# The first weight unit of a two-layer decoder by pairs of feature tiles, and the norm's weights on ScalarE's queue

## The chip, the cores and the metric

The kernel runs as one program on 1 core of one Trainium2 chip. The metric is device time in microseconds (us) of one execution; the kernel before was run three times and its median is used. Times inside an execution are counted from the start of the profiled span. PE is TensorE, ACT ScalarE, DVE VectorE, POOL GpSimd, SP SyncE; SP's queue issues nearly all transfers.

## What is computed

Two layers of a hybrid decoder over 256 tokens of 1024 features, in float32. Each layer is a half SwiGLU block, a token mixer (windowed attention beside a gated recurrence in layer 0, a chunked delta rule in layer 1), cross-attention into 256 memory tokens, and another half SwiGLU block, each behind an RMSNorm. The part that the change touches is the very first block:

```python
def rmsnorm(x, g):
    y = x * rsqrt(mean(x * x, axis=-1, keepdims=True) + 1e-6)
    return y * g

def swiglu(h, w_in, w_out):              # w_in: 1024 x 5632, w_out: 2816 x 1024
    gate, up = split(h @ w_in, 2, axis=-1)
    return (silu(gate) * up) @ w_out

x = x + 0.5 * swiglu(rmsnorm(x, ffn1_norm[0]), ffn1_w_in[0], ffn1_w_out[0])
```

## The kernel before

Every weight matrix is cut into units of 256 columns by up to 1024 rows (eight feature tiles k of 128). A unit is loaded in two halves of four tiles, 512 KB each, into a ring of `RAW` = 5 raw buffers (`load_to`), and each half is split (`split_half`, lines 158 and 159): ACT copies the weights rounded into `wt[..., 0, :]`, the high part, and DVE subtracts that from the raw weights to get the low part `wt[..., 1, :]`. Activations are kept transposed, features on partitions, and split in the same way: `x2[:, k, 0]` high and `x2[:, k, 1]` low.

`mm3` makes one product of a unit's column half j (128 columns) over some tiles k. For each k it issues two matmuls: `high` (line 200), the weights' high part against both parts of the activations side by side, 512 columns wide, and `low` (line 204), the weights' low part against the activations' high part, 256 columns wide. For the last k the low comes first. A pair in the texts below is one high with its low; a unit has 16 of them. Eight tiles accumulate in one PSUM bank per j. Outside the start, `tick` splits the next half while a unit's products run, and a list `plan` with its `queue` of halves sets the order of the weights. Line 271 (`add`) and line 270 then fold a finished bank's two halves together in SBUF.

The start is in `setup`, inside `tc.manual_schedule()`: there each engine issues its instructions in the order written. Outside that region the scheduler orders them, by its own estimate of what is ready when.

- The gains of the first norm are read as rows into `dcw` (128 rows of 512 B, line 467, on SP's queue), transposed on PE (line 483) and copied to `gains` (line 484).
- x comes in four pieces of 256 features, 256 KB each, into `xs` (lines 473 and 477). For each piece c, `transposed` (line 429) makes four transposes on PE, and `take` (lines 503 and 506) multiplies by the gains and splits: ACT makes the high part of both feature tiles, DVE the low part. The mean of squares is not needed for this: its reciprocal root is applied after the products.
- `idle(n)` (line 491) issues n matmuls of a matrix of ones that nobody reads.
- The loads stand in this order on SP's queue: dcw, x's pieces 0 and 1, unit 0's first half (in two transfers), unit 1's first half, x's pieces 2 and 3, then the second halves of units 0 and 1, then unit 2's first half. The queue of halves is swapped for this (line 75).
- PE's order: `idle(7)`, the gains, piece 0's transposes, `idle(3)`, piece 1's transposes, `idle(6)`, unit 0's products over tiles 0 to 3, the transposes of pieces 2 and 3, unit 1's over 0 to 3, then the second halves of both units.
- Behind the products ACT squares x with a running sum (line 535), DVE copies the transposed x from PSUM to `xT` (line 537) and scales the sums to `ms` (line 366), POOL takes the power -1/2 into `rcol` (line 341), and PE transposes that to a row (`stats_rows`, line 374). These transposes stand on PE behind the products of units 0 and 1 and ahead of unit 2.

Of the kernel before, what the change touches and what calls it, by code (L numbers as in the profile page):

```python
# [9 lines left out]
F32 = mybir.dt.float32  # L10
# [3 lines left out]
AF = mybir.ActivationFunctionType  # L14
# [4 lines left out]
P = 128  # L19
S = 256  # L20
D = 1024
KD = 8
# [45 lines left out]
class Net:  # L68
    def __init__(self, tc, t):
        self.tc, self.nc, self.t = tc, tc.nc, t  # L70
        self.raws, self.halves = {}, {}
        self.plan = list(self.make_plan())
        self.queue = [(i, k) for i, u in enumerate(self.plan) for k in range(0, u[4], 4)]

        self.queue[1], self.queue[2] = self.queue[2], self.queue[1]
        self.n_load = self.n_half = self.n_take = 0
        self.later = deque()
        self.banks, self.n_bank = "w", 0
        self.now, self.due = 0, []
# [46 lines left out]
            yield from four("xa_wo", l)  # L126
            yield from ffn(2, l)

    def load_to(self, n, step=4):

        nc = self.nc
        while self.n_load < min(n, len(self.queue)):
            i, k = self.queue[self.n_load]
            name, l, c0, k0, nk, cols = self.plan[i]
            m = min(4, nk - k)
            raw = self.p_raw.tile([P, 4, 256], F32, name="raw")
            src = self.t[name][l, (k0 + k) * P:(k0 + k + m) * P, c0:c0 + cols]
            src = src.rearrange("(k p) c -> p k c", p=P)
            for u in range(0, m, step):
                us = slice(u, min(m, u + step))  # L140
                nc.sync.dma_start(raw[:, us, :cols], src[:, us])
            self.raws[self.n_load] = raw
            self.n_load += 1

    def split_half(self, step=4):

        nc = self.nc
        i, k = self.queue[self.n_half]
        name, l, _, _, nk, cols = self.plan[i]
        self.load_to(self.n_half + 1)  # L150
        n = min(4, nk - k)
        wt = self.p_wt.tile([P, 4, 2, 256], F32R, name="wt")
        raw = self.raws.pop(self.n_half)
        self.n_half += 1
        for u in range(0, n, step):
            us = slice(u, min(n, u + step))
            a, b, r = wt[:, us, 0, :cols], wt[:, us, 1, :cols], raw[:, us, :cols]
            nc.scalar.activation(a, r, AF.Copy)  # L158
            nc.vector.tensor_sub(b, r, a.bitcast(F32))  # L159
        self.halves.setdefault(i, []).append(wt)  # L160

    def w(self, name, c0):

# [23 lines left out]

    def mm3(self, out, wts, cols, mov, ks, k0=0, start=0, stop=KD):  # L190

        nc = self.nc
        for k in ks:
            i = k - k0
            w = wts[i // 4][:, i % 4]

            def high():
                nc.tensor.matmul(out.rearrange("p a s -> p (a s)"), w[:, 0, cols], mov[:, k].rearrange("p a s -> p (a s)"),  # L200
                                 start=k == start, stop=k == stop - 1)

            def low():
                nc.tensor.matmul(out[:, 0], w[:, 1, cols], mov[:, k, 0], start=False, stop=False)  # L204

            for part in (low, high) if k == stop - 1 else (high, low):
                part()

# [223 lines left out]
    def setup(self, ctx):  # L432
        nc, tc, t = self.nc, self.tc, self.t
# [8 lines left out]
        c = self.p_c  # L442
# [11 lines left out]
        self.dcw = c.tile([P, P], F32, name="dcw")  # L454

        warm = c.tile([P, 1], F32, name="warm")
        nc.scalar.activation(warm, self.ones[:, :1], AF.Silu)
        x_pool = tc.tile_pool(name="xs", bufs=1, reuse_waits="tile")
        xs = x_pool.__enter__().tile([P, 2, D], F32, name="xs")
        x = t["x"][0].rearrange("(t p) d -> p t d", p=P)  # L460
        spare = self.p_sm.tile([P, S], F32, name="acc", bufs=2)
        rows0, rows, rows2 = self.dcw, spare[:, :P], spare[:, P:]

        def put(dst, r0, name, eng, n=None, times=1):
            ap = t[name]
            n = n or math.prod(ap.shape) // P
            eng.dma_start(dst[r0:r0 + n * times],
                          bass.AP(tensor=ap.tensor, offset=ap.offset, ap=[[0, times], [P, n], [1, P]]))

        put(rows0, 0, "ffn1_norm", nc.sync, times=8)  # L470

        for a, b in ((0, 256), (256, 512)):
            nc.sync.dma_start(xs[:, :, a:b], x[:, :, a:b])
        self.load_to(1, 2)
        self.load_to(2)
        for a, b in ((512, 768), (768, 1024)):
            nc.sync.dma_start(xs[:, :, a:b], x[:, :, a:b])
        self.load_to(RAW)
        xs = [xs[:, j] for j in range(2)]

        def columns(dst, src, which="s"):
            ps = self.bank(which)
            nc.tensor.transpose(ps[:, 0, :P], src, self.ident)
            nc.vector.tensor_copy(dst, ps[:, 0, :P])

        with tc.manual_schedule():

            def idle(n):
                ps = self.bank("w").rearrange("p a s -> p (a s)")
                for _ in range(n):  # L490
                    nc.tensor.matmul(ps[:, :P], self.ones, self.ones, start=True, stop=True)

            idle(7)
            gains = self.p_sm.tile([P, 1, S], F32, name="bc", bufs=2)[:, 0, :P]
            columns(gains, rows0, "w")
            banks = []

            def take(ks, ps):
                banks.append((ks, ps))
                g = lambda k: gains[:, C_FFN1 + k:C_FFN1 + k + 1]  # L500
                for j in range(2):
                    k = ks.start + j
                    nc.scalar.activation(self.x2[:, k, 0], ps[:, j], AF.Copy, scale=g(k))
                for j in range(2):
                    k = ks.start + j
                    nc.vector.scalar_tensor_tensor(self.x2[:, k, 1], ps[:, j], g(k), self.x2[:, k, 0].bitcast(F32),
                                                   op0=OP.mult, op1=OP.subtract)


            self.first = [[self.bank(w) for w in u] for u in ("ww", "ws")]  # L510

            def products(u, half, j):
                self.mm3(self.first[u][j], self.halves[u], slice(j * P, j * P + P), self.x2,
                         range(4 * half, 4 * half + 4))

            self.transposed(xs, take, (0,))
            idle(3)
            self.transposed(xs, take, (1,))
            idle(6)
            self.split_half(2)  # L520
            products(0, 0, 0)
            self.split_half()
            products(0, 0, 1)
            self.transposed(xs, take, (2, 3))
            products(1, 0, 0)
            products(1, 0, 1)
            for u in range(2):
                self.split_half(2)
                for j in range(2):
                    products(u, 1, j)  # L530
            self.load_to(4 + RAW)
            ms = self.p_sm.tile([P, 2], F32, name="ms", bufs=2)
            for j in range(2):
                junk = self.m2[:, 2 * j:2 * j + 2].rearrange("p k a s -> p (k a s)")
                nc.scalar.activation(junk, xs[j], AF.Square, accum_out=ms[:, j:j + 1])
            for ks, ps in banks:
                nc.vector.tensor_copy(self.xT[:, ks], ps)
# [939 lines left out]
```

## Time and profile before

| | |
|---|---|
| three runs | 1252.36, 1251.72 and 1255.6 us, median 1252.36 |
| profiled execution | 1251.99 us, its span 1250.2 us |
| PE busy | 1236.0 us, 99% of the span |
| DVE, ACT, POOL busy | 929.0, 752.0 and 80.5 us |
| moved by DMA | 222.92 MB, mean 178 GB/s |
| mean granted TensorE clock | 0.998 |

A row of a timeline has the start in us, the duration in us, the engine, the line of the kernel, the operation, output and input, and how many like instructions are merged in the row; in brackets stand the idle time of the engine ahead of it and what ended that. Matmuls overlap, so a row's duration is longer than its distance to the next. A row of a waits view has who waited for whom, the total in us, the number of times and the longest. A row of the DMA issues has the count, the size of one and, where the trace has it, the median time in us from issue to landing.

### The profile page before, as it was taken

The numbers are of one execution on the slowest core, as the hardware profiler recorded it, in microseconds if no ns is written. First come the engines' busy times: TensorE is split into PE (matmuls) and PEld (weight loads), VectorE is DVE, ScalarE is ACT, GpSimd is POOL, SyncE is SP. The second block draws the span as 40 slices with busy tenths as digits, with TensorE's granted clock in tenths as the row PEclk, the third lists the DMA queues.
The fourth block names the chain that finished last, engine by engine and source line by source line (L and its number), as shares of the span: only waits on it lengthen the run. The fifth ranks groups of instructions, "written<-read, shape, count | busy, mean of one in ns | idle before, by whom it ended". The sixth has DMA issues, their size and how long they took to land.

```text
span 1250.2 us, 20300 instructions
## 1 busy us (share of the span) xinstructions
PE 1236.0 (99%) x7702; PEld 1104.9 (88%) x7702; DVE 929.0 (74%) x1590; ACT 752.0 (60%) x1281; POOL 80.5 (6%) x96
## 2 busy tenths in 40 slices
PE   9999999999999999999999999999999999999997
PEld 8888889888998888888888888888898998888887
DVE  6987957788668778766877756989757668777753
ACT  7766545886555665545656544776757465666543
POOL 1000020000101000011000001020001101000000
PEclk9999999999999999999999999999999999999999
DMA  8766676544544566557666566667534535666561
GB/s 272 215 206 197 185 255 185 178 125 152 185 135 154 185 198 184 183 185 231 187 187 195 181 192 204 183 153 193 142 99 135 181 124 169 185 186 194 177 194 60
DMA packets 231019, 222.92 MB, mean 178 GB/s; under 512 B 14969, under 2 KB 228617, under 8 KB 230793
## 3 DMA queue, kind: packets, MB, share of 16 engines
q1 hardware_dynamic: 229448, 217.94, 56.9%
q0 software_dynamic: 1152, 3.15, 1.0%
q8 instruction: 60, 0.98, 0.3%
q10 hardware_dynamic: 320, 0.53, 0.1%
q14 instruction: 39, 0.31, 0.1%
HBM read 215.03 MB, written 5.51 MB: 176 GB/s over the span
## 4 chain that ended last, share of the span: by engine, by line
PE 90%; DVE 5%; ACT 2%; DMA 1%; issue 1%; POOL 1%; ACTq 0%; DVEq 0%; POOLq 0%
PE psw L200 21%; PE pss L200 16%; PE psw L204 11%; PE psf L200 11%; PE pss L204 8%; PE psf L204 5%; PE psw L242 5%; PE psf L242 4%; PE pss L242 3%; PE psw L216 2%; DVE wt L159 1%; PE psw L220 1%; ACT wt L158 1%; PE pss L1268 1%; PE psf L1274 1%
## 5 line engine op out<-in xcount | busy, mean ns | idle before, releaser
L159 DVE TENSOR_TENSOR wt<-raw,wt 128x1024 fp32r<-128x1024 f32 (+1 forms) x409 | 484.9, 1191 | 202.8 <-ACT wt L158 199.6
L158 ACT ACTIVATE wt<-raw 128x1024 fp32r<-128x1024 f32 (+1 forms) x409 | 418.6, 1031 | 172.1 <-PE psw L204 59.4
L200 PE MATMUL psw<-x,wt 128*128 128x512 f32 x864 | 310.6, 396 | 2.1 <-DVE xn L271 1.8
L204 PE MATMUL psw<-x,wt 128*128 128x256 f32 x864 | 224.9, 281 | 0.5 <-DVE wt L159 0.5
L200 PE MATMUL pss<-x,wt 128*128 128x512 f32 x520 | 187.4, 393 | 0.0
L200 PEld LDWEIGHTS psw<-x,wt 128*128 128x128 f32 x864 | 160.6, 188 | 30.1 <-issue 2.1
L204 PEld LDWEIGHTS psw<-x,wt 128*128 128x128 f32 x864 | 162.4, 188 | 9.4 <-DVE wt L159 1.0
L204 PE MATMUL pss<-x,wt 128*128 128x256 f32 x520 | 134.9, 280 | 0.0
L200 PE MATMUL psf<-x,wt 128*128 128x512 f32 x352 | 127.2, 394 | 0.0
L200 PEld LDWEIGHTS pss<-x,wt 128*128 128x128 f32 x520 | 97.7, 188 | 16.9 <-ACT bc L377 0.4
L204 PEld LDWEIGHTS pss<-x,wt 128*128 128x128 f32 x520 | 97.7, 188 | 5.4
L200 PE MATMUL psw<-h,wt 128*128 128x512 f32 x264 | 94.9, 396 | 0.0
L204 PE MATMUL psf<-x,wt 128*128 128x256 f32 x352 | 91.3, 280 | 0.0
L200 PE MATMUL pss<-h,wt 128*128 128x512 f32 x242 | 87.0, 396 | 0.0
L336 POOL TENSOR_TENSOR acc<-acc,sq 128x256 f32<-128x256 f32 x49 | 43.7, 891 | 658.3 <-ACT sq L334 557.3
L200 PEld LDWEIGHTS psf<-x,wt 128*128 128x128 f32 x352 | 66.1, 188 | 11.2
L204 PE MATMUL psw<-h,wt 128*128 128x256 f32 x264 | 72.0, 280 | 0.0
L204 PEld LDWEIGHTS psf<-x,wt 128*128 128x128 f32 x352 | 66.2, 188 | 3.5
L204 PE MATMUL pss<-h,wt 128*128 128x256 f32 x242 | 66.0, 280 | 0.0
L200 PEld LDWEIGHTS psw<-h,wt 128*128 128x128 f32 x264 | 49.6, 188 | 10.8
L200 PE MATMUL psf<-h,wt 128*128 128x512 f32 x154 | 55.4, 397 | 0.0
L200 PEld LDWEIGHTS pss<-h,wt 128*128 128x128 f32 x242 | 45.5, 188 | 9.8
(377 smaller groups left out, 2109.2 us busy)
## 6 DMA issues: line engine op xcount, KB each, us to landing
raw<-in_ffn_w_in_dram SPq DMA_DIRECT2D x175, 512.0 KB, 3.6
raw<-in_ffn_w_out_dram SPq DMA_DIRECT2D x80, 512.0 KB, 3.6
raw<-in_xa_wkv_dram SPq DMA_DIRECT2D x32, 512.0 KB, 3.5
raw<-in_dn_w_in_dram SPq DMA_DIRECT2D x32, 512.0 KB, 4.6
raw<-in_ab_w_in_dram SPq DMA_DIRECT2D x20, 512.0 KB, 3.6
raw<-in_xa_wq_dram SPq DMA_DIRECT2D x16, 512.0 KB, 3.5
raw<-in_xa_wo_dram SPq DMA_DIRECT2D x16, 512.0 KB, 3.4
raw<-in_ffn_w_out_dram SPq DMA_DIRECT2D x16, 256.0 KB, 2.9
```

What stands on the lines that cost most here:

```text
L158: nc.scalar.activation(a, r, AF.Copy)
L159: nc.vector.tensor_sub(b, r, a.bitcast(F32))
L200: nc.tensor.matmul(out.rearrange("p a s -> p (a s)"), w[:, 0, cols], mov[:, k].rearrange("p a s -> p (a s)"), start=k == start, stop=k == ...
L204: nc.tensor.matmul(out[:, 0], w[:, 1, cols], mov[:, k, 0], start=False, stop=False)
L216: nc.tensor.matmul(out.rearrange("p a s -> p (a s)"), mov[:, k, 0, tok], w.rearrange("p a s -> p (a s)"), start=k == 0, stop=k == KD - 1)
L220: nc.tensor.matmul(out[:, 0], mov[:, k, 1, tok], w[:, 0], start=False, stop=False)
L242: self.nc.tensor.matmul(out, a[u], b[w], start=first and i == 0, stop=last and i == 2)
L336: (eng or nc.gpsimd).tensor_add(self.acc, self.acc, sq)
L1268: nc.tensor.matmul(py[:, i], na[:, i], tu[:, 0, i], start=True, stop=True)
L1274: nc.tensor.matmul(pp[:, i], yy[:, i], tu[:, 1, i], start=True, stop=True)
```

## The change

`load_pair(n)` loads two feature tiles (256 KB) of unit 0, and `setup` now alternates: x's piece n, then the weights' tiles 2n and 2n + 1, for n from 0 to 3. Unit 1's halves and unit 2's first half follow; the swap of the queue is gone, so a unit's halves are neighbours. The splits become a generator, `split_steps`, which gives control back after each piece of two tiles. PE's order becomes: `idle(5)`, the gains, piece 0's transposes, `idle(3)`, and then three times the transposes of the next piece and the products of the pair of tiles before it over both j, and behind them the last pair; with `late=True` the four highs of a pair stand before its four lows. Unit 1 follows as two whole halves, each split in one piece. `idle(6)` is gone. The load of `dcw` moves from SP's queue to ACT's, ahead of the activation that warms up ACT's table.

```diff
--- before.py
+++ after.py
@@ -71,8 +71,6 @@
         self.raws, self.halves = {}, {}
         self.plan = list(self.make_plan())
         self.queue = [(i, k) for i, u in enumerate(self.plan) for k in range(0, u[4], 4)]
-
-        self.queue[1], self.queue[2] = self.queue[2], self.queue[1]
         self.n_load = self.n_half = self.n_take = 0
         self.later = deque()
         self.banks, self.n_bank = "w", 0
@@ -126,7 +124,16 @@
             yield from four("xa_wo", l)
             yield from ffn(2, l)
 
-    def load_to(self, n, step=4):
+    def load_pair(self, n):
+
+        name, l, c0, _, _, cols = self.plan[0]
+        if n % 2 == 0:
+            self.raws[n // 2] = self.p_raw.tile([P, 4, 256], F32, name="raw")
+        src = self.t[name][l, 2 * n * P:(2 * n + 2) * P, c0:c0 + cols].rearrange("(k p) c -> p k c", p=P)
+        self.nc.sync.dma_start(self.raws[n // 2][:, 2 * n % 4:2 * n % 4 + 2, :cols], src)
+        self.n_load = n // 2 + 1
+
+    def load_to(self, n):
 
         nc = self.nc
         while self.n_load < min(n, len(self.queue)):
@@ -136,13 +143,14 @@
             raw = self.p_raw.tile([P, 4, 256], F32, name="raw")
             src = self.t[name][l, (k0 + k) * P:(k0 + k + m) * P, c0:c0 + cols]
             src = src.rearrange("(k p) c -> p k c", p=P)
-            for u in range(0, m, step):
-                us = slice(u, min(m, u + step))
-                nc.sync.dma_start(raw[:, us, :cols], src[:, us])
+            nc.sync.dma_start(raw[:, :m, :cols], src)
             self.raws[self.n_load] = raw
             self.n_load += 1
 
-    def split_half(self, step=4):
+    def split_half(self):
+        self.run(self.split_steps(4))
+
+    def split_steps(self, step):
 
         nc = self.nc
         i, k = self.queue[self.n_half]
@@ -152,12 +160,13 @@
         wt = self.p_wt.tile([P, 4, 2, 256], F32R, name="wt")
         raw = self.raws.pop(self.n_half)
         self.n_half += 1
+        self.halves.setdefault(i, []).append(wt)
         for u in range(0, n, step):
             us = slice(u, min(n, u + step))
             a, b, r = wt[:, us, 0, :cols], wt[:, us, 1, :cols], raw[:, us, :cols]
             nc.scalar.activation(a, r, AF.Copy)
             nc.vector.tensor_sub(b, r, a.bitcast(F32))
-        self.halves.setdefault(i, []).append(wt)
+            yield
 
     def w(self, name, c0):
 
@@ -187,7 +196,7 @@
 
 
 
-    def mm3(self, out, wts, cols, mov, ks, k0=0, start=0, stop=KD):
+    def mm3(self, out, wts, cols, mov, ks, k0=0, start=0, stop=KD, only=""):
 
 
 
@@ -203,6 +212,9 @@
             def low():
                 nc.tensor.matmul(out[:, 0], w[:, 1, cols], mov[:, k, 0], start=False, stop=False)
 
+            if only:
+                (high if only == "high" else low)()
+                continue
             for part in (low, high) if k == stop - 1 else (high, low):
                 part()
 
@@ -454,10 +466,6 @@
         self.dcw = c.tile([P, P], F32, name="dcw")
 
         warm = c.tile([P, 1], F32, name="warm")
-        nc.scalar.activation(warm, self.ones[:, :1], AF.Silu)
-        x_pool = tc.tile_pool(name="xs", bufs=1, reuse_waits="tile")
-        xs = x_pool.__enter__().tile([P, 2, D], F32, name="xs")
-        x = t["x"][0].rearrange("(t p) d -> p t d", p=P)
         spare = self.p_sm.tile([P, S], F32, name="acc", bufs=2)
         rows0, rows, rows2 = self.dcw, spare[:, :P], spare[:, P:]
 
@@ -467,14 +475,15 @@
             eng.dma_start(dst[r0:r0 + n * times],
                           bass.AP(tensor=ap.tensor, offset=ap.offset, ap=[[0, times], [P, n], [1, P]]))
 
-        put(rows0, 0, "ffn1_norm", nc.sync, times=8)
-
-        for a, b in ((0, 256), (256, 512)):
-            nc.sync.dma_start(xs[:, :, a:b], x[:, :, a:b])
-        self.load_to(1, 2)
-        self.load_to(2)
-        for a, b in ((512, 768), (768, 1024)):
-            nc.sync.dma_start(xs[:, :, a:b], x[:, :, a:b])
+        put(rows0, 0, "ffn1_norm", nc.scalar, times=8)
+        nc.scalar.activation(warm, self.ones[:, :1], AF.Silu)
+        x_pool = tc.tile_pool(name="xs", bufs=1, reuse_waits="tile")
+        xs = x_pool.__enter__().tile([P, 2, D], F32, name="xs")
+        x = t["x"][0].rearrange("(t p) d -> p t d", p=P)
+
+        for n in range(4):
+            nc.sync.dma_start(xs[:, :, n * 256:n * 256 + 256], x[:, :, n * 256:n * 256 + 256])
+            self.load_pair(n)
         self.load_to(RAW)
         xs = [xs[:, j] for j in range(2)]
 
@@ -490,7 +499,7 @@
                 for _ in range(n):
                     nc.tensor.matmul(ps[:, :P], self.ones, self.ones, start=True, stop=True)
 
-            idle(7)
+            idle(5)
             gains = self.p_sm.tile([P, 1, S], F32, name="bc", bufs=2)[:, 0, :P]
             columns(gains, rows0, "w")
             banks = []
@@ -506,28 +515,30 @@
                     nc.vector.scalar_tensor_tensor(self.x2[:, k, 1], ps[:, j], g(k), self.x2[:, k, 0].bitcast(F32),
                                                    op0=OP.mult, op1=OP.subtract)
 
-
             self.first = [[self.bank(w) for w in u] for u in ("ww", "ws")]
 
-            def products(u, half, j):
-                self.mm3(self.first[u][j], self.halves[u], slice(j * P, j * P + P), self.x2,
-                         range(4 * half, 4 * half + 4))
-
+            def products(u, ks, late=False):
+                js = [slice(j * P, j * P + P) for j in range(2)]
+                for which in ("high", "low") if late else ("",):
+                    for j in range(2):
+                        self.mm3(self.first[u][j], self.halves[u], js[j], self.x2, ks, only=which)
+
+            def weights():
+                for _ in range(2):
+                    yield from self.split_steps(2)
+
+            w0 = weights()
             self.transposed(xs, take, (0,))
             idle(3)
-            self.transposed(xs, take, (1,))
-            idle(6)
-            self.split_half(2)
-            products(0, 0, 0)
-            self.split_half()
-            products(0, 0, 1)
-            self.transposed(xs, take, (2, 3))
-            products(1, 0, 0)
-            products(1, 0, 1)
-            for u in range(2):
-                self.split_half(2)
-                for j in range(2):
-                    products(u, 1, j)
+            next(w0)
+            for n in range(3):
+                self.transposed(xs, take, (n + 1,))
+                products(0, range(2 * n, 2 * n + 2), late=True)
+                next(w0)
+            products(0, range(6, 8))
+            for half in range(2):
+                self.split_half()
+                products(1, range(4 * half, 4 * half + 4))
             self.load_to(4 + RAW)
             ms = self.p_sm.tile([P, 2], F32, name="ms", bufs=2)
             for j in range(2):
```

## The prediction

> **What bounds the kernel now.** I read the page first: engine totals, and the chain of work that ended last.
>
> ```profile
> PE 1236.0 (99%) x7702; PEld 1104.9 (88%) x7702; DVE 929.0 (74%) x1590; ACT 752.0 (60%) x1281; POOL 80.5 (6%) x96
> PE 90%; DVE 5%; ACT 2%; DMA 1%; issue 1%; POOL 1%; ACTq 0%; DVEq 0%; POOLq 0%
> ```
>
> TensorE is busy for 99% of the span and is 90% of the chain. So a change of the start can only win what PE does at the start that is no product, and the win stays if the rest can start earlier too. The busy times by stretch say which engines could forbid that.
>
> ```profile
> 9.87:21.90 12.03, 12.03 (x71) 10.49 (x71) 9.23 (x18) 9.38 (x19) 2.62 (x3) 1.00 0.87 270
> 21.90:40.00 18.10, 18.06 (x104) 15.51 (x104) 17.83 (x28) 13.67 (x24) 1.78 (x1) 1.00 0.97 308
> ```
>
> Columns: stretch, length, busy PE, PE loads, DVE, ACT, POOL, granted clock, DMA share, GB/s. From 9.87 on PE hardly stops. DVE is nearly full from 21.90 to 40, but has 2.8 us free in the stretch before. The third view is PE in order of time (start, duration, line).
>
> ```profile
> 1.05 3.35 PE L491 MATMUL psw<-ones 128*128 128x128 f32 x14 [1.05 <-DVE mhalf L452]
> 4.20 0.42 PE L483 MATMUL psw<-ident,dcw 128*128 128x128 f32 x1
> 4.43 1.12 PE L429 MATMUL psf<-ident,xs 128*128 128x128 f32 x4
> 5.34 1.49 PE L491 MATMUL psw<-ones 128*128 128x128 f32 x6
> 6.62 0.81 PE L429 MATMUL pss<-ident,xs 128*128 128x128 f32 x4
> 7.27 1.50 PE L491 MATMUL psw<-ones 128*128 128x128 f32 x12
> 8.88 0.50 PE L200 MATMUL psw<-x,wt 128*128 128x512 f32 x1
> 9.87 0.39 PE L204 MATMUL psw<-x,wt 128*128 128x256 f32 x1 [0.49 <-DVE wt L159]
> 10.10 0.39 PE L200 MATMUL psw<-x,wt 128*128 128x512 f32 x1
> 12.53 0.60 PE L429 MATMUL psf<-ident,xs 128*128 128x128 f32 x4
> 12.97 0.60 PE L429 MATMUL pss<-ident,xs 128*128 128x128 f32 x4
> 17.17 0.40 PE L204 MATMUL psw<-x,wt 128*128 128x256 f32 x2
> 17.41 0.62 PE L200 MATMUL psw<-x,wt 128*128 128x512 f32 x2
> 21.90 0.43 PE L374 MATMUL pss<-ident,rcol 128*128 128x128 f32 x2
> ```
>
> L491 is idle work on ones; beside it PE only transposes up to 8.88. The products of units 0 and 1, 32 pairs of a high (L200) and a low (L204), run from 8.88 to L374, the row-sum transposes, at 21.90. Seven pairs lie between 10.10 and 12.53: 0.347 us a pair. Two lows in a row start 0.12 apart (17.17 to 17.41), so sorting highs before lows costs nothing.
>
> What runs beside: the loads, ACT, DVE and POOL, from their timelines; the fourth row is the mean GB/s of each microsecond from 0 to 40.
>
> ```profile
> 0.74 0.80 SPq L467 DMA_DIRECT2D dcw<-in_ffn_norm_dram  x1
> 1.60 0.93 SPq L473 DMA_DIRECT2D xs<-in_x_dram  x2
> xs<-in_x_dram SPq DMA_DIRECT2D x1, 256.0 KB, 2.8
> GB/s 0 0 83 320 239 246 325 337 342 320 366 362 350 342 333 282 279 317 24 8 194 383 376 350 348 283 386 358 365 201 315 230 267 342 345 316 280 282 300 187
> 0.73 1.28 ACT L457 ACT_TABLE_LOAD   x1 [0.73 <-PEq L1464]
> 7.47 0.84 ACT L503 ACTIVATE x<-pss,bc 128x256 fp32r<-128x256 f32 x2 [1.04 <-PE pss L429]
> 8.34 0.88 DVE L506 SCALAR_TENSOR_TENSOR x<-pss,bc,x 128x256 fp32r<-128x256 f32 x2 [1.01 <-ACT x L503]
> 14.61 2.20 ACT L158 ACTIVATE wt<-raw 128x512 fp32r<-128x512 f32 x4
> 15.62 2.49 DVE L159 TENSOR_TENSOR wt<-raw,wt 128x512 fp32r<-128x512 f32 x4
> 16.70 1.07 ACT L535 ACTIVATE m<-xs 128x1024 fp32r<-128x1024 f32 x1
> 18.68 0.21 ACT L535 ACTIVATION_READ_ACCUMULATOR m<-xs 128x1 f32 x1
> 18.02 0.68 DVE L537 COPY xT<-psf 128x512 f32<-128x512 f32 x1
> 20.42 0.57 DVE L366 TENSOR_SCALAR ms<-ms 128x2 f32<-128x2 f32 x1
> 21.14 0.71 POOL L341 TENSOR_TENSOR rcol<-ms,mhalf 128x2 f32<-128x2 f32 x1 [0.18 <-DVE gs L271]
> 21.98 1.22 DVE L159 TENSOR_TENSOR wt<-raw,wt 128x1024 fp32r<-128x1024 f32 x1
> ```
>
> **The change, part by part.** Times below are on this trace's clock; T0 to T3 are the transposes of a feature pair, P0 to P3 unit 0's products of it.
>
> *Norm weights on ACT's queue.* SP's first issue, 0.74, becomes x's first piece instead of dcw. With its 2.8 us to landing that is 3.54; at worst it shares the engines with dcw and lands as before, at 4.40. I take 4.0, a little nearer the worse end because the same 64 KB flow beside it. ACT issues dcw at 0.73; at SP's 0.80 us its table load and warm-up go back to about 3.0, while ACT's first real work follows T0, so that costs nothing. If it took longer, up to 2 us would still be hidden. The issue itself is saved on SP for every later load, but these wait for bandwidth, which stays as it is.
>
> The Trainium skill ("DMA: Bandwidth & Descriptors", "Issuing engines are not separate DMA queues") says that transfers from different issuers share the same engines and only issue time is saved. By it x's first piece shares with dcw and lands at the worse end, 4.40: P0 would start at 7.25 and the sum be 1.85 instead of 2.1 us. No row here has both queues at work, so I leave it there.
>
> *PE until the first product.* idle(5) ends at 1.05 + 5 x 0.45 = 3.3 (seven took 1.05 to 4.20). Then the gains' transpose, and T0 at 4.0, lasting 0.91 (4.43 to 5.34): 4.9. idle(3) takes 1.28: 6.2. T1 takes 0.65 (6.62 to 7.27), if x's second piece is there. It is the third transfer now: 66 + 3 x 262 = 852 KB. The GB/s row sums to 888 KB by 6.0, so 852 stand at 5.85; x's first piece had its last byte (328 KB) at about 3.8 and was used at 4.43, 0.6 later; hence 6.45, or 0.3 less as the bytes start sooner. P0 starts at 7.0 (6.85 to 7.1; with a tail twice as long, 7.7). idle(6), 1.6 us, is gone.
>
> *Splits and products by pairs.* Splits of 128x512 cost ACT 0.53 and DVE 0.62 each back to back (2.20 and 2.49 for four), as many as before for unit 0; of unit 1's halves one is split whole today already and the other in two pieces; both are whole now. DVE's whole half takes 1.22 by its row (21.98), against 2 x 0.62; for ACT I take 2 x 0.53. Taking a feature pair: ACT 0.84, DVE 0.85 after it.
> PE: P0 to 8.4 (four pairs, 1.39); T2 (0.44, 12.53 to 12.97) and P1 to 10.2; T3 and P2 to 12.05. Feeding this: T3 ends at 10.65, ACT takes to 11.55, DVE to 12.45, its split to 13.05. P2's feed, one round earlier, is ready at 10.6 against a start of 10.65. P3 waits: its first high goes at 12.45 and its first low at 13.05, then 1.16: 14.2, 0.8 lost. Loads: the seventh and eighth pieces (1.9 and 2.16 MB) are in at about 9.6 and 10.4 by the same row, before T3 at 10.2 and ACT's split at 11.55.
> Unit 1: 16 x 0.347 = 5.55, so 19.8. ACT splits its halves from 12.15 and 13.4 (3.21 MB by 12.8, plus 0.6), ending 14.45; DVE follows to 15.6. PE's first low there, 14.45, finds DVE's first half done at 14.4.
>
> *Behind it.* L374 waits for a chain that PE just meets today: ACT's squares end at 18.89 (18.68 + 0.21), POOL's pow comes at 21.14, and PE goes on at 21.90, 3.01 us behind the squares. The squares now start at 14.45 and take 2.2 (16.70 to 18.89): 16.65, so 19.66. DVE: 15.6, four copies (18.02 to 20.42, 2.4), the scale: 18.6, no hindrance. PE is ready at 19.8. **Sum:** L374 goes from 21.90 to 19.8, 2.1 us earlier. DVE's copies move from 18.02 to 15.6, 2.4 earlier, so the full DVE stretch behind can follow. Raw buffers come free earlier as well, which closes the hole in the loads at 18 to 20 us (24 and 8 GB/s).
>
> The profiled execution took 1251.99; less 2.1 it is 1249.9. The median, 1252.36, is 0.37 above it, so I predict 1250.3. The bounds of the start (P0 at 6.85 to 7.7) give 2.25 to 1.4 us; with the scatter of runs, 1249.2 to 1251.2 for this case.
>
> **Rivals.**
>
> *A. The gains come late, slower.* T0 stands behind the gains' transpose. T0 may slip to 4.3 before T1 moves; from there each microsecond costs one. The gain is gone when dcw takes 5.4 us from issue.
>
> ```profile
> acc<-in_ffn_norm_dram SPq DMA_DIRECT2D x2, 8.0 KB, 5.4
> raw<-in_ffn_w_in_dram SPq DMA_DIRECT2D x3, 512.0 KB, 8.1
> out_dram<-raw ACTq DMA_DIRECT2D x2, 256.0 KB, 2.3
> ```
>
> The same tensor with the queue full took 5.4, and the longest load near the start 8.1: then T0 is at 9.1, 4.8 later than 4.3, less 2.1: 2.7 us slower, 1255.1. Against it: on the empty queue dcw was in by 4.20, 3.46 after issue, and ACT's own transfers land in 2.3. Chance 0.07.
>
> *B. PE is still at half pace when the products start.* Six idle records take 1.49 us at 5.34 and twelve 1.50 at 7.27: the pace doubles near 7.1, though the clock column says 1.00 throughout. Now PE stands still from 3.3 to about 3.9. If the 6.1 us of work that it took count from there, the doubling comes at 10.0; 3 us of products at half pace lose 1.5: 1251.8. For it: fewer idle matmuls; against it: the work between 4 and 7 is as dense as before. Chance 0.14.
> The Trainium skill ("TensorE: Matmul & The Clock Gate", Part 1) has a free-running window of about 3.4 us that must be busy; a missed one would cost 1.7 us, 1252.0. The trace's 6.1 us from the first matmul is later than one window.
>
> *C. The gain turns into a wait.* L374 has 0.15 us to spare, and DVE is 17.83 of 18.10 busy afterwards. If ACT's squares or DVE's splits come no earlier than today, all 2.1 us are lost: 1252.4. It needs unit 1's second half to land 2 us later than worked out. Today's wait at that place and the longest later:
>
> ```profile
> PE pss L374 <- POOL rcol L341: 0.2, 1, 0.2
> PE psw L200 <- DVE xn L271: 1.8, 1, 1.8
> ```
>
> Chance 0.13.
>
> *D. The order of work behind the region is drawn anew.* Outside it the instructions aren't in the order written: SP issues norm loads, written after the weight loads, ahead of them.
>
> ```profile
> 8.46 1.30 SPq L467 DMA_DIRECT2D acc<-in_ffn_norm_dram  x1
> 12.51 1.86 SPq L141 DMA_DIRECT2D raw<-in_ffn_w_in_dram  x2
> ```
>
> One wait like the 1.8 us more or less: 1252.1 or 1248.5. Chance 0.08.
>
> **How the numbers follow.** My forecast has 0.58. The range 1248.8 to 1253.0 takes in its own range with some scatter, B, C and D's upper end, and leaves out A and D's lower end. 0.3% is 3.8 us, about what a measurement here can tell from no change; the gain can't reach that, since with P0 at 6.85, 32 pairs in 11.1, T2 and T3 in 0.9 and no wait at all L374 would be at 18.85, 3.05 us earlier. Faster 0.05 (D, scatter), slower 0.05 (A's far end, scatter), within 0.90.
>
> **What would show it.** Right: dcw issued by ACT near 0.73; T0 near 4.0; the first L200 near 7.0 at full pace; a PE wait of some 0.4 us twice, on DVE, before unit 0's last pair; L374 near 19.8; no hole in the loads around 18 us. Wrong: T0 past 4.4 behind L483 (A); products 0.7 us a pair after 7.2 (B); a long wait of L374 on POOL or new waits on L159 after it (C); new PE waits past 40 us (D).

## The result and the profile after

| | before | after |
|---|---|---|
| median of six runs, us | 1252.41 (1251.72 to 1256.03) | 1260.76 (1259.08 to 1262.91) |
| ratio | | 1.0057, interval 1.0044 to 1.0071 |
| profiled execution, its span, us | 1251.99, 1250.2 | 1259.08, 1257.3 |
| mean granted clock of that execution | 0.998 | 0.996 |

The change costs about 8 us, where 2 us less had been forecast. Two executions among the runs below, 2472.32 us of e2 and 3145.81 us of the kernel before, lie so far out that they stand in no comparison; their cause is open. From the page of the kernel after: the engine totals and the row of the granted clock.

```profile
PE 1237.3 (98%) x7686; PEld 1105.9 (88%) x7686; DVE 928.7 (74%) x1589; ACT 752.1 (60%) x1280; POOL 80.1 (6%) x96
PEclk9999999999999999999999999989999999999999
```

PE is busy 1.3 us longer with less work to do, and one slice of 40 has an 8 in the clock row: the 27th (817 to 849 us). The start isn't there.

To find the place, take a PE instruction that occurs once in every block: the transposes of the row sums (`stats_rows`, L374 before, L386 after). Six of them cut the span.

| start of the transposes, us | 1 | 2 | 3 | 4 | 5 | 6 | end of span |
|---|---|---|---|---|---|---|---|
| before | 21.90 | 204.14 | 409.79 | 594.53 | 776.88 | 1064.25 | 1250.2 |
| after | 22.20 | 204.04 | 409.66 | 594.40 | 776.75 | 1071.90 | 1257.3 |

Up to the fifth the two kernels are within 0.3 us of each other. The whole loss lies between the fifth and the sixth: the delta rule and the cross-attention of layer 1, which the diff doesn't mention. Their row in the view by stretches, before and then after:

```profile
776.88:1064.25 287.37, 282.40 (x1946) 258.42 (x1946) 222.21 (x488) 188.94 (x389) 30.98 (x32) 1.00 0.54 156
```

```profile
776.75:1071.90 295.15, 285.33 (x1946) 261.01 (x1947) 222.64 (x488) 189.41 (x389) 30.48 (x32) 0.99 0.52 152
```

The same 1946 matmuls keep PE busy 2.9 us longer, and PE stands idle for 9.8 instead of 5.0 us. So the 7.8 us are 4.9 of waits and 2.9 of matmuls at a lower pace. PE's waits after, from 776 to 945 us, and the rows around the longest:

```profile
PE psf L1208 <- DVE y L1092: 2.7, 1, 2.7
PE psw L228 <- DVE wt L168: 1.9, 1, 1.9
PE pss L1114 <- ACT th L1108: 1.3, 1, 1.3
PE pss L1359 <- DVE qk L1350: 1.1, 1, 1.1
PE pss L1291 <- DVE tu L1286: 0.8, 1, 0.8
```

```profile
815.37 2.60 ACT L1136 ACTIVATE e<-e,ngc 128x128 f32<-128x128 f32 x8 [3.67 <-DMA e<-gd]
817.88 0.61 ACT L1091 ACTIVATE th<-y 128x512 f32<-128x512 f32 x1
818.52 0.69 DVE L1092 SCALAR_TENSOR_TENSOR y<-th,y 128x512 f32<-128x512 f32 x1 [1.12 <-ACT th L1091]
819.27 1.16 PE L1208 MATMUL psf<-y 128*128 128x128 f32 x8 [2.73 <-DVE y L1092]
821.61 0.77 PE L209 MATMUL psw<-x,wt 128*128 128x512 f32 x1
822.39 0.63 PE L209 MATMUL psw<-x,wt 128*128 128x512 f32 x1
```

ACT stands 3.7 us until a transfer brings `e`, does eight exponentials in a row, then the silu of the queries; DVE multiplies; only then can PE go on. Before, PE waits 1.8 us in this stage (the L200 on `xn` of the prediction) and 1.0 for `qk`, and not for the other four. Behind the wait highs stand some 0.64 us apart instead of 0.35. The granted clock after, and before in the same stretch:

```profile
820.00:825.00 5.00, 5.00 (x23) 4.52 (x23) 4.36 (x12) 4.76 (x13) 1.18 (x1) 0.56 0.41 116
825.00:830.00 5.00, 5.00 (x24) 4.32 (x24) 3.91 (x8) 2.86 (x5) 0.00 (x0) 0.76 0.70 166
```

```profile
820.00:825.00 5.00, 4.38 (x31) 4.11 (x32) 4.70 (x14) 5.00 (x12) 0.00 (x0) 1.00 0.84 210
```

Two causes are to be found: why the order in the delta rule differs, and why the clock falls.

**The order.** PE's instructions of both kernels, laid side by side in order, differ at the start and in the two mixers, and agree in the feed-forward blocks. The line that does this is the new `split_half`. It drains the generator by `run`, and `run` calls `tick` after every step:

```python
def run(self, gen):
    while True:
        try: next(gen)
        except StopIteration as e: return e.value
        self.tick()

def tick(self):
    if self.n_half < len(self.queue) and self.queue[self.n_half][0] <= self.n_take:
        self.split_half()
    if self.later:
        self.later.popleft()()
    self.now += 1
    while self.due and self.due[0][0] <= self.now:
        self.due.pop(0)[2]()
```

A tick is the unit of time in which the mixers order their work: `self.after(n, fn)` runs `fn` n ticks later, and the constants `EXP`, `KST`, `QST`, `AB` are counts of ticks. Before, a unit gives four ticks; now each split of a half also ticks, six in all. So everything that is due comes about 1.5 times as early, measured in units of products.

### The profile page after: what moved, and what is told of

Same layout as the page of the kernel before. It is cut to its first block, busy times and chain, and to the rows that moved or that the text cites. A ratio compares the mean times of both kernels' runs of the same rounds, so it can differ in the third digit from the quotient of the medians.

```text
span 1257.3 us, 20280 instructions
## 1 busy us (share of the span) xinstructions
PE 1237.3 (98%) x7686; PEld 1105.9 (88%) x7686; DVE 928.7 (74%) x1589; ACT 752.1 (60%) x1280; POOL 80.1 (6%) x96
## 5 line engine op out<-in xcount | busy, mean ns | idle before, releaser
L168 DVE TENSOR_TENSOR wt<-raw,wt 128x1024 fp32r<-128x1024 f32 (+1 forms) x408 | 484.7, 1192 | 201.1 <-ACT wt L167 198.7
```

## The experiments

Letters in the expectations: K, the tick in `split_half` is the cause (K1 by its count of due work, K2 by its splitting the next half early); X, within K1 the exponentials alone; Y, several due pieces together; Q, the queries alone; C, part of the price is the fall of the clock behind a wait. The kernel before ran beside each of three batches, on three chips: medians 1254.32 (e1 to e4), 1253.82 (e5 to e7 and e9) and 1253.52 (e10 to e12). Each ratio is against the kernel before of the same batch; it need not be the quotient of the two medians. The executions of before can be told apart by their mean clock: of 79, 46 have 0.998 or more and a median of 1252.83, and 33 have 0.997 or less and a median 3.2 us longer, 1255.98.

**e1_no_tick**: the change without the tick.

```diff
 def split_half(self):
-    self.run(self.split_steps(4))
+    for _ in self.split_steps(4):
+        pass
```

> The changed kernel, but each whole half is split without calling run(), so that no split calls tick(); the start by pairs is kept. Theory K (the extra ticks cost the time): the gated delta rule's stage takes as long as before, so 1252.4 us, ratio 1.000 within 0.002, with the second last row-sum transposes (776.7 before and after) and the last ones (1064.2 before, 1071.9 after) at 1064 to 1065. Theory L (the new start does it, by loads or buffers that stand otherwise for the rest of the kernel): still 1259 to 1262.

Measured: 1253.04 us, ratio 0.9985 (0.9973 to 0.9997). Its stage, and its longest wait there:

```profile
776.55:1064.46 287.91, 282.09 (x1945) 258.41 (x1946) 222.11 (x488) 189.07 (x389) 30.91 (x32) 1.00 0.54 156
```

```profile
PE psw L210 <- DVE xn L284: 1.8, 1, 1.8
```

One call less in the helper gives the loss back, 0.72% or 9.0 us between the two ratios. The stage takes 287.9 us as it did before (287.4), its longest wait is the 1.8 us of before, and the clock is 1.00. Behind the first 50 us PE's instructions stand in the order of before. What is left, the change as it was described, is worth 1.9 us (0.4 to 3.4).

**e2_tick_only**, **e3_clock_only**, **e4_halves_only**: the kernel before, with the whole tick added at the end of `split_half`, or only its count, or only its early split.

```diff
 # e2, before's split_half
+    if self.n_take:
+        self.tick()
 # e3
+    if self.n_take:
+        if self.later:
+            self.later.popleft()()
+        self.now += 1
+        while self.due and self.due[0][0] <= self.now:
+            self.due.pop(0)[2]()
 # e4
+    if self.n_take and self.n_half < len(self.queue) and self.queue[self.n_half][0] <= self.n_take:
+        self.split_half()
```

> The kernel before, with one call of tick() at the end of every split outside the start; the start, its loads and its queue are untouched. Theory K: 1259 to 1262 us, with the waits of the changed kernel in the delta rule's stage (2.7 us on DVE's y, 1.9 us on wt). Theory L: 1252.4.

> The kernel before, with only the clock's part of tick() after every split outside the start: now goes up, due and later work is called; no further half is split. If the faster clock of the due work is what costs (K1): 1258 to 1262. If it is that both halves of a unit are split at once (K2): 1252.4.

> The kernel before, with only the splitting part of tick() after every split outside the start: the next half is split at once if its unit is due, and the clock does not move. K1: 1252 to 1253. K2: 1258 to 1262. If both parts count, each gives a part of the 8.4 us.

Measured: e2 1262.53, ratio 1.0052 (1.0033 to 1.0071); e3 1261.41, 1.0050 (1.0031 to 1.0068); e4 1254.87, 1.0002 (0.9988 to 1.0016). The tick alone, in a kernel whose start is untouched, brings the loss; its count alone brings it whole; the early split brings nothing measurable. K1 holds, K2 falls. The waits expected of e2 can't be read: its profile is of the execution of 2472.32 us, in which PE is busy for 2462.9 us instead of 1236.0 with the same 7702 matmuls. e3's longest wait stands at the place of L1208 above (L1203 in its file), followed by a longer fall of the clock:

```profile
PE psf L1203 <- DVE y L1087: 4.5, 1, 4.5
```

```profile
820.00:825.00 5.00, 2.30 (x11) 2.30 (x11) 4.10 (x10) 4.88 (x15) 0.00 (x0) 0.62 1.10 276
825.00:830.00 5.00, 5.00 (x17) 4.30 (x18) 3.91 (x10) 3.88 (x8) 1.03 (x1) 0.50 0.58 144
```

**e5_exp_late**, **e6_exp_early**, **e10_query_late**: which due work? The change with the exponentials due later; the kernel before with them earlier; the change with the queries' steps later.

```diff
 # e5, after             # e6, before            # e10, after
-EXP = (16, 17, 22, 23) -EXP = (16, 17, 22, 23) -QST = (2, 9, 5)
+EXP = (19, 22, 28, 30) +EXP = (13, 14, 18, 19) +QST = (2, 13, 7)
```

> The changed kernel, fast clock kept, with the four exponentials of the decay alone due later: EXP = (19, 22, 28, 30) instead of (16, 17, 22, 23). In the changed kernel ACT stands 3.7 us before the first of them for its transfer and then does 8 in a row, and the silu that the query products need waits behind. Theory X (this early exp is the link): the 2.7 us wait at the query products falls under 1.8, the pace stays full, 1253 to 1257. Rival Y (all due work is too early, no one step decides): 1258 to 1262, with another wait of over 2 us.

> The kernel before, with EXP = (13, 14, 18, 19) instead of (16, 17, 22, 23) and nothing else. X: ACT is held some 4 us longer (three ticks of 1.4 us), PE's wait behind it grows from 1.8 to over 3 us, the pace halves for some us: 1257 to 1263. Y: 1252 to 1255.

> The changed kernel with the query products alone due later, QST = (2, 13, 7) instead of (2, 9, 5), which is where the faster clock took them from by a factor of about 1.5. Theory Q (PE comes to the first query products a half unit too early, with nothing else in its queue to do while ACT stands for the decay's transfer): no wait of 2.7 us there, a clock of 0.997 or more, 1254 to 1257, ratio 1.001 to 1.004. Rival Y (several steps are early, each finds its own wait): ratio 1.004 to 1.007, and another wait of 2 us or more in the same place.

Measured: e5 1259.82, ratio 1.0047 (1.0031 to 1.0062); e6 1256.55, 1.0024 (1.0010 to 1.0039); e10 1258.43, 1.0033 (1.0020 to 1.0046). The waits of e5 and e10:

```profile
PE psf L1208 <- DVE y L1092: 2.8, 1, 2.8
PE pss L1279 <- ACT tu L1292: 1.8, 1, 1.8
PE psw L228 <- DVE ti L1246: 1.7, 1, 1.7
```

```profile
PE psf L1208 <- DVE y L1092: 2.7, 1, 2.7
PE psw L209 <- DVE xn L283: 1.9, 1, 1.9
```

In neither profile is the wait at L1208 gone, and neither edit gives the loss back, so neither the exponentials nor the queries are the whole cause. They are not nothing either. Exponentials that come early cost before 3 us, about half of what the whole count costs it (e3): a wait of 2.6 us on `th`, and the clock at 0.62. Late queries save 0.24%, or 3 us, against the change, and a ratio of 1.0033 lies in the range that had been expected for Q; e10's profile shows its longest execution (1262.14 us, mean clock 0.995), while six of its nine have 0.998 or more, so the wait in those is not known. Y, several due pieces together, fits best. But no run moves the exponentials and the queries together, or the other counts (`KST`, `VST`, `AB`), so which pieces matter, and how much each, stays open.

**e7_filled**: the change, with ten idle matmuls behind the last product ahead of the queries' products, into a bank that these overwrite. (`self.last` is the last matmul that `mm3` issued.)

```diff
+                    if p == 0:
+                        with tc.issue_after(self.last.ins):
+                            for _ in range(10):
+                                nc.tensor.matmul(kq[:, 0], self.ones, self.ones, start=True, stop=True)
```

> The changed kernel, with ten idle matmuls of ones (2.5 us) written into the bank of the first query products just ahead of them, so that PE works in the place where it stands still for 2.7 us. If the halved pace after that wait is part of the price (theory C): no slow stretch there, mean clock back to 0.997 or more, some 3 to 4 us less than the changed kernel, 1255 to 1258. If PE's pace has another cause: 1260 to 1263, as the idle work gains nothing.

Measured: 1258.16, ratio 1.0031 (1.0019 to 1.0042), 0.26% or 3.3 us below that of the change, whose interval begins at 1.0044. The clock of the stretch:

```profile
820.00:825.00 5.00, 5.00 (x36) 4.66 (x37) 3.91 (x9) 4.53 (x11) 1.22 (x1) 1.00 0.24 67
```

So C has a part: filling the wait keeps the clock at 1.00 where it was 0.56. The size agrees with the 2.9 us of the view by stretches, though the two intervals only just miss each other, so it is known to some 2 us only. The order of the stage moved by half a unit here too (the wait at that place is now 1.4, on `na`), so it isn't a clean subtraction.

**e9_keep_clock** and **e12_before_keep**: seven idle matmuls behind the last product at tick 20 of the delta rule, in e1 and in the kernel before.

```diff
+            def keep():
+                ps = self.bank("s")
+                with tc.issue_after(self.last.ins):
+                    for _ in range(7):
+                        nc.tensor.matmul(ps[:, 0, :P], self.ones, self.ones, start=True, stop=True)
+
+            self.after(20, keep)
```

> The kernel of e1_no_tick, with seven idle matmuls (1.75 us) queued behind the last product of tick 20 of the delta rule, in the place where PE stands 1.8 us for DVE. The runs of the kernel before fall into two groups, at a clock of 0.998 to 1.000 (1252 to 1254) and of 0.996 to 0.997 (1255 to 1258). Theory C (that wait halves the pace in some runs): one group at 0.998 or more, median 1250 to 1252, ratio 0.997. If the slow group has another cause: two groups as before, 1253, or 1254 to 1255 if the idle work costs its own time.

> The kernel before with the seven idle matmuls of e9_keep_clock and nothing of the change. If the idle work alone removes the slow group of runs: 1252.5, ratio 0.998 to 0.999, and the new start is worth what is left to e9_keep_clock (0.998), some 0.05 to 0.1%. If it is the start that gave the gain: ratio 1.000.

Measured: e9 1251.91, ratio 0.9981 (0.9970 to 0.9992); e12 1252.45, 0.9980 (0.9966 to 0.9995). The waits on `xn` at that place, 1.8 us before and in e1, are now 0.2 in e9 and 0.9 in e12:

```profile
PE psw L210 <- DVE xn L284: 0.2, 1, 0.2
```

```profile
PE psw L200 <- DVE xn L271: 0.9, 1, 0.9
```

All 12 runs of e12 and 10 of 11 of e9 have a mean clock of 0.998 or more, against 46 of 79 of before. e12 differs from before in nothing but the idle work, so the 3.2 us that before loses in some executions are tied to the wait at this place, behind which the clock sometimes falls. Before was profiled only in an execution without such a fall. The profile of e4 (1257.27 us) has one, and from the fifth landmark up to this place e4's engines do the same work in the same order:

```profile
PE psw L202 <- DVE xn L273: 2.4, 1, 2.4
```

```profile
825.00:830.00 5.00, 5.00 (x20) 4.57 (x21) 5.00 (x11) 4.93 (x15) 0.00 (x0) 0.54 0.64 168
```

There ACT stood 4.50 us for the transfer of `e` instead of 3.95, and PE 2.4 us for `xn` instead of 1.8: the wait itself is not the same in every execution. Idle work alone gives the kernel before as much as the new start and the idle work together; beside it the start's share can't be resolved.

**e11_dcw_sp**: e9, with `dcw` back on SP's queue, behind x's first piece.

```diff
-        put(rows0, 0, "ffn1_norm", nc.scalar, times=8)
         nc.scalar.activation(warm, self.ones[:, :1], AF.Silu)
 ...
             nc.sync.dma_start(xs[:, :, n * 256:n * 256 + 256], x[:, :, n * 256:n * 256 + 256])
+            if n == 0:
+                put(rows0, 0, "ffn1_norm", nc.sync, times=8)
             self.load_pair(n)
```

> The kernel of e9_keep_clock with the gains' rows back on SP's queue, behind x's first piece. If the load on ACT's queue holds up the first transposes (PE waited 0.8 to 1.0 us for it): they start at about 4.0 instead of 4.4 to 4.5, the row sums' transposes come up to 0.5 us earlier, 1250 to 1252, ratio 0.997 to 0.999. If the start is bound by x's second piece and the loads behind it: no change against e9_keep_clock (0.998).

Measured: 1251.07, ratio 0.9979 (0.9968 to 0.9990), the lowest median of all, but not to be told from e9. Its start is no earlier; at the second landmark it stands 1.3 us behind e9 (204.33 against 203.01):

```profile
4.86 0.45 PE L494 MATMUL psw<-ident,dcw 128*128 128x128 f32 x1 [1.30 <-DMA dcw<-in_ffn_norm_dram]
22.46 0.38 PE L387 MATMUL pss<-ident,rcol 128*128 128x128 f32 x2
```

The gains still land last and PE waits for them, on either queue.

## Why the prediction was wrong, step by step

**The step that failed** is "Splits and products by pairs", where the splits were costed by their durations alone ("as many as before"). It took `split_half` through `split_steps` as the same instructions in another form. They are; but draining them by `run` advances a count that orders the two mixers, and that was read nowhere, although the diff shows the call. The step belongs in the sum with +6.3 us (e3 against before) to +9.0 us (the change against e1) instead of 0. The bound of "at most 3.05 us earlier" and the range were both bounds of the start, the wrong place.

**Rival D** had the right place, the order of work behind the region, with a chance of 0.08. Its reason was not the right one: it is no estimate of the scheduler that changed but the order in which the program issues its work. Its price, one wait of 1.8 us, was short as well: several waits together take 4.9, and the clock takes another 2.9 (2.9 and 3.3 by two views).

**The start.** The steps in the profiles of the change and of e7, which has the same start:

| | predicted | after | e7 |
|---|---|---|---|
| T0, us | 4.0 | 4.76 | 4.31 |
| first high of unit 0 | 7.0 | 7.61 | 6.96 |
| row-sum transposes | 19.8 | 22.20 | 20.55 |

```profile
0.74 1.26 ACTq L475 DMA_DIRECT2D dcw<-in_ffn_norm_dram  x1
4.52 0.45 PE L492 MATMUL psw<-ident,dcw 128*128 128x128 f32 x1 [0.97 <-DMA dcw<-in_ffn_norm_dram]
4.76 1.06 PE L441 MATMUL psf<-ident,xs 128*128 128x128 f32 x4
7.61 1.46 PE L209 MATMUL psw<-x,wt 128*128 128x512 f32 x4
14.65 0.50 PE L213 MATMUL psw<-x,wt 128*128 128x256 f32 x2 [0.43 <-DVE wt L168]
15.00 1.06 ACT L167 ACTIVATE wt<-raw 128x1024 fp32r<-128x1024 f32 x1 [0.45 <-DMA raw<-in_ffn_w_in_dram]
20.37 1.21 DVE L168 TENSOR_TENSOR wt<-raw,wt 128x1024 fp32r<-128x1024 f32 x1
20.38 1.77 POOL L353 TENSOR_TENSOR rcol<-ms,mhalf 128x2 f32<-128x2 f32 x1 [0.18 <-DVE gs L283]
22.20 0.43 PE L386 MATMUL pss<-ident,rcol 128*128 128x128 f32 x2 [0.55 <-POOL rcol L353]
```

```profile
4.31 1.06 PE L441 MATMUL psf<-ident,xs 128*128 128x128 f32 x4
6.96 1.22 PE L209 MATMUL psw<-x,wt 128*128 128x512 f32 x4
20.55 0.43 PE L386 MATMUL pss<-ident,rcol 128*128 128x128 f32 x2 [0.15 <-POOL rcol L353]
```

- *Norm weights on ACT's queue*: the issue took 1.26 us, not 0.80, and the gains, not x, are what PE waits for (0.97). T0 stands at 4.31 to 5.12 in the six profiles with this load on ACT's queue. So rival A's mechanism is there, at a price of 0 to 0.8 us behind its 4.3 instead of 4.8.
- *PE until the first product*: right in e7 (6.96 against 7.0), 0.6 late in the profile of the change, where T0 is 0.8 late.
- *The pace at the start* (rival B): in the change's profile four highs take 1.46 us, in e7 1.22, in e1 2.06, so the doubling comes between 7 and 10 us and differs from run to run. From the first high of P0 to the first of P1 the three take 2.5, 1.9 and 3.1 us, so B cost about 0.5 us in the change's profile (0.17 of its 0.6 is a wait for x) and 1.2 in e1: it is right in some executions.
- *The wait before unit 0's last pair*: 0.43 us on the split, once, where two of some 0.4 had been predicted.
- *Loads*: unit 1's second half landed at 15.0, predicted 13.4, and the hole in the loads did not close: it moved from 18 to 20 us to 17 to 19 (14 and 69 GB/s in the change's profile).
- *Behind it*: POOL's power took 1.77 instead of 0.71 us, beside a subtraction on DVE that started with it (see the last section); with 0.71 it would have ended at 21.09, ahead of PE's last product (21.65), and the 0.55 us of wait would be gone.

Over all, the start gives less than the 2.1 us: at the second landmark the six kernels with the new start and the gains on ACT's queue stand at 203.39 on the mean (after, e1, e5, e7, e9, e10; 202.80 to 204.04), the five with the old one at 204.31 (before, e3, e4, e6, e12; 204.14 to 204.55): 0.9 us. The time of e1 allows that and the 2.1 (0.4 to 3.4).

## What to carry to other kernels

Where a kernel spreads work by a count of steps, every call that advances the count is part of the schedule: before costing a refactor at nothing, follow the helper to what else it does, and compare the order of instructions outside the edited region. When a loss appears, find its place with one instruction that recurs in every block before explaining anything; here two rows showed that the loss did not lie at the start. A wait on TensorE can cost twice, by its length and by the pace behind it, and a few idle matmuls in it are cheap.

## What the runs showed of the hardware

- **The pace falls behind shorter waits than I had thought.** In this stage the granted clock fell in the profiles behind waits of 2.4 (e4), 2.6 (e6), 2.7 (after, e10), 2.8 (e5) and 4.5 us (e3), and behind no wait of less than 1.8. At 1.8 to 1.9 us both happened: it fell behind 1.8 on `tu` in e5 and 1.9 on `xn` in e10, and stayed at 1.00 behind 1.8 in before and e1 and 1.9 on `wt` in after and e7. Added up from windows of 1 us, the time at half clock is 3.4 us (twice in e5, once in e10), 6.8 (after, e4, e6, e10) or 10.2 (e3), always a multiple of 3.4. The Trainium skill ("TensorE: Matmul & The Clock Gate", "HAM oscillation") names idle gaps above some 3.4 us as the ones to avoid; all of these falls but e3's came behind shorter ones, so here the measurement decides.
- **POOL stands still beside a subtraction on DVE.** The power took 0.71 us in e1 and before, 1.77 and 1.79 in the change and e7, where DVE's L168 begins at the same time; in the change it starts 0.01 us behind DVE's L168 (20.37 to 21.58) and ends 0.57 us after that. In e1 the same subtraction begins 0.17 us behind the power and doesn't lengthen it, so what counts is which of the two is first. The Trainium skill ("SBUF — State Buffer", "SBUF: two separate sides") says that an operation of VectorE with two inputs from SBUF and one of GpSimd that reads SBUF exclude each other for a whole instruction; the trace agrees with it. The trace of before has it too, in a like power at 33.66 us that took 1.78; the prediction had read only the short one.
